# Two heads' scores and transposes, issued turn by turn on the two row halves of TensorE

## The chip, the core and the metric

The kernel runs on one core of one Trainium2 chip, as one program. The metric is the device time of an execution in microseconds; the median of three executions of the kernel before is 3099.32 us. Five engines work side by side, each through its own queue in order: TensorE (PE, with its weight loads as PEld), VectorE (DVE), ScalarE (ACT), GpSimd (POOL) and SyncE (SP), which here issues nearly all DMAs.

## What is computed

Two layers of a decoder trunk on 1024 tokens of width 1024, in float32. Layer 0 has a gated linear recurrence (Hawk) as its mixer, layer 1 RWKV-7 time mixing; each is followed by a SwiGLU block and a gated per-layer embedding. The change lies in the RWKV-7 recurrence, 16 heads of 64 channels:

```python
def step(S, inp):
    r_t, w_t, k_t, v_t, a_t, b_t = inp
    sa = jnp.einsum('bhvk,bhk->bhv', S, a_t)
    S = S * w_t[:, :, None, :] + sa[..., None] * b_t[:, :, None, :] + v_t[..., None] * k_t[:, :, None, :]
    y = jnp.einsum('bhvk,bhk->bhv', S, r_t)
    return S, y
```

The kernel doesn't step through tokens. It cuts the sequence in chunks of 64 tokens and computes, per chunk and head, the 64x64 matrices of scores between tokens, the inverse of a triangular one of them, and with these the state's step from chunk to chunk.

## The kernel before

Tokens are worked on in two halves of 512 (`t`), features lie on the partitions. The dense products (names `pg`, `pu`, `ops`, `pps`, `lps`, `lx`, `gx`, `pq`) each add up three float32r matmuls of 128x512 per block of weights, from a high and a low part of both operands. Weights are loaded by SyncE into `raw`, ScalarE casts the high part `whl` (L238) and GpSimd subtracts for the low one (L239).

The recurrence is woven into this dense work. A group `G` is four heads of a half, that is two pairs `jj` of heads; the two heads of a pair lie on partitions 0 to 63 (`E`) and 64 to 127 (`O`), and `HV` lists them. Four generators produce the work:

- `stage1` prepares a pair: decays, `BK` and `ZL`, then for each half of its eight chunks the scores `sc` (L115 by way of `mm`): four products of 64 rows by 128 columns per head, into one PSUM bank of 128x512. VectorE masks the bank in three steps, into AB, RB and ZL (L1057 to L1059). Then `bkt` (L1079): eight transposes per head into one bank, which ScalarE copies to `BKt` (L1083).
- `inverse` inverts the triangular matrices of a group: a long chain of small steps on VectorE (`X`, `W`), then `w`, `n`, `u`, `w`, `v`, 32 small products each, into banks of the same kind.
- `stage2` goes from chunk to chunk with `zu` and `y`, which have PSUM of their own. Its products already alternate between `E` and `O`.
- `norm2` normalizes with `bsum` and `yv`, into banks of the same kind, and stores the output `o`.

There are two such banks (`BANKS = 2`); `big` hands them out in turn. The order of TensorE's instructions in this part is fixed as the code emits them; the other engines are ordered by a scheduler with priorities (`ahead`). What the code emits is decided by a planner in the class `Kern`. It keeps a clock in ns, to which `mm` adds the length of each product. After each dense matmul `tick` looks at the four generators. Each has yielded a triple: a latency from its last step, which is multiplied by a slack of 3 (2.5 in the last part), whether it needs a bank, and a condition. A generator whose latency is over, whose bank (the next in turn) is planned free and whose condition holds is stepped, and no other follows for 1200 ns of that clock. `evac` plans a bank free after the time given with `big`, again times the slack. These plans set the order alone; on the chip, semaphores hold an instruction until its bank is really empty.

When the generators have ended, the memory pool of the scan is closed, and pools `ep` and `pe` with weight buffers and PSUM take its place (`K.until(lambda: not K.streams)`, `c.close()`, `extra(ctx)` in `tile_trunk`).

Of the kernel before, what the change touches and what calls it, by code (L numbers as in the profile page):

```python
# [27 lines left out]
BANKS = 2  # L28
# [25 lines left out]
class Part:  # L54
    def __init__(self, gen):
        self.gen, self.need = gen, (0.0, False, None)


class Kern:
# [61 lines left out]
    def ready(self, st):  # L121
        lat, bank, cond = st.need
        return (cond is None or cond()) and max(lat, self.bank_free[self.bank_n % BANKS] if bank else 0.0)
# [809 lines left out]
    def scan(self):  # L933
# [41 lines left out]
        def evac():  # L975

            i, t = held.pop(0)
            self.bank_free[i] = self.clock + t * self.slack
# [11 lines left out]
        def stage1():  # L990
# [15 lines left out]
            for P, (t, g, jj) in enumerate(order):  # L1006
# [23 lines left out]
                for c4 in range(0, NC, 4):  # L1030
# [18 lines left out]
                    yield 1500, True, None  # L1049
                    for hh, me, ot in HV:  # L1050
                        ps = big("sc", 1700).rearrange("p (c s) -> p c s", c=4)
                        for c in range(4):
                            self.mm(ps[:, c, :], BK[me, c4 + c, :, :].rearrange("p i s -> p (i s)"), zl[me, hh, c, :])
                        evac()
                        m3 = mask.unsqueeze(1).to_broadcast([128, 4, 128])
                        with self.ahead(AHEAD_S1):
                            nc.vector.tensor_mul(AB[me, cs, :], ps[me, :, 0:64], m3[me, :, 0:64])  # L1057
                            nc.vector.tensor_mul(rb[me], ps[me, :, 64:128], m3[me, :, 64:128])
                            nc.vector.tensor_mul(zl[ot, hh], ps[ot], m3[ot])  # L1059
                        if hh == 0:  # L1060
                            yield 0, True, None
                yield 0, True, (lambda: (G == 0 or inv[G - 1] >= 1) and (old < 0 or s2[old] == NC))
# [13 lines left out]
                for hh, me, ot in HV:  # L1076
                    ps = c3(big("bkt", 800))
                    for c in range(NC):
                        nc.tensor.transpose(ps[:, c, :], BK[me, c, :, :].rearrange("p i s -> p (i s)"), ident[me])  # L1079
                    self.clock += NC * 54  # L1080
                    evac()
                    with self.ahead(AHEAD_S1):
                        nc.scalar.copy(BKt[:, :, hh, :], ps)  # L1083
                    if hh == 0:
                        yield 0, True, None
# [366 lines left out]
```

## Time and profile before

| | |
|---|---|
| median of three runs | 3099.32 us (3097.59 to 3109.37) |
| the profiled execution: time, span | 3106.82 us, 3105.0 us |
| its mean granted TensorE clock | 0.979 of 2.4 GHz |
| TensorE busy | 2958.3 us, 95% of the span |
| VectorE, ScalarE, GpSimd busy | 1677.9, 1438.3, 1282.7 us |
| stretch of the woven recurrence | about 1130 to 2480 us |

A busy share is the part of the span in which an engine had an instruction running. TensorE's matmuls are pipelined, so their records overlap; a group's cost is read from the start of what stands before it to the start of what comes behind it. A float32 product leaves two records, a transpose or a float32r product one. In a list of waits, each row says who sat idle, until what ended, for how long in total, how often, and the longest time.

### The profile page before, as it was taken

The page shows a single profiled execution, that of the slowest core. Times are in us where ns is not written, and L with a number is a line of the kernel's source. Part 1 is how long each engine was busy: PE and PEld are TensorE (multiplying, and loading weights), DVE is VectorE, ACT ScalarE, POOL GpSimd, SP SyncE. Part 2 cuts the span into 40 slices and gives each one's busy share as a digit, 9 for nine tenths or more (in the row PEclk, how much of TensorE's full clock was granted, in tenths as well). Part 3 has the DMA queues.
Part 4 walks back from the last instruction along what each step waited for, and adds up shares of the span by engine and source line. Part 5 has one row for each costly group of instructions (what it writes and reads, how often), then busy time and mean ns, then how long its engine had stood idle before and what let it go on. Part 6 is the DMA issues. An engine that isn't in the chain of part 4 may idle for free. (4 is left out here: it accounts for less than half of the span.)

```text
span 3105.0 us, 45886 instructions
## 1 busy us (share of the span) xinstructions
PE 2958.3 (95%) x16904; PEld 2292.7 (74%) x16904; DVE 1677.9 (54%) x2950; ACT 1438.3 (46%) x2565; POOL 1282.7 (41%) x1080
## 2 busy tenths in 40 slices
PE   5999999999999999999998999999999999999998
PEld 3777778888776777777776667776767777888886
DVE  8756771111563266576678565777866456222145
ACT  5564752222555443444465774454344445322244
POOL 5111134444445444343434344434333355544445
PEclk9999999999998999999999999999999999999999
DMA  3211123333335464333323366423323252333323
GB/s 126 60 36 53 50 79 105 94 94 95 98 126 179 158 190 128 89 111 98 114 91 98 119 204 198 125 85 111 100 88 100 70 185 91 103 95 95 95 81 109
DMA packets 223968, 336.04 MB, mean 108 GB/s; under 512 B 56960, under 2 KB 75136, under 8 KB 223744
## 3 DMA queue, kind: packets, MB, share of 16 engines
q1 hardware_dynamic: 223456, 332.75, 34.9%
q8 instruction: 133, 2.18, 0.3%
q14 instruction: 91, 0.75, 0.1%
q10 hardware_dynamic: 288, 0.37, 0.0%
HBM read 278.24 MB, written 54.79 MB: 107 GB/s over the span
## 5 line engine op out<-in xcount | busy, mean ns | idle before, releaser
L239 POOL TENSOR_TENSOR whl<-raw,whl 128x512 fp32r<-128x512 f32 (+2 forms) x818 | 1061.8, 1303 | 1410.4 <-ACT whl L238 1319.8
L238 ACT CAST whl<-raw 128x512 fp32r<-128x512 f32 (+2 forms) x818 | 482.2, 593 | 851.5 <-PE ops L115 226.2
L115 PE MATMUL ops<-hid,whl 128*128 128x512 f32 x2112 | 523.8, 401 | 13.8 <-DVE hid L290 6.4
L115 PE MATMUL pg<-xn,whl 128*128 128x512 f32 (+1 forms) x2184 | 522.9, 392 | 4.4 <-ACT whl L238 1.9
L115 PEld LDWEIGHTS pg<-xn,whl 128*128 128x128 f32 x2184 | 405.2, 188 | 98.9 <-issue 4.3
L115 PEld LDWEIGHTS ops<-hid,whl 128*128 128x128 f32 x2112 | 392.6, 189 | 113.8 <-DVE hid L290 12.5
L115 PE MATMUL pu<-xn,whl 128*128 128x512 f32 x1584 | 385.9, 396 | 3.1 <-ACT xn L289 1.4
L115 PEld LDWEIGHTS pu<-xn,whl 128*128 128x128 f32 x1584 | 296.0, 189 | 72.0 <-DVE xn L290 2.1
L115 PE MATMUL pps<-mix,whl 128*128 128x512 f32 x1152 | 301.3, 412 | 11.9 <-ACT mix L289 5.1
L390 DVE TENSOR_TENSOR h<-h,ops 128x512 f32<-128x512 f32 x256 | 173.9, 685 | 210.6 <-PE ops L115 208.7
L555 DVE TENSOR_TENSOR sg<-sg,pu 128x512 f32<-128x512 f32 x88 | 60.4, 686 | 396.0 <-PE pu L115 395.4
L115 PEld LDWEIGHTS pps<-mix,whl 128*128 128x128 f32 x1152 | 217.7, 193 | 75.1 <-issue 7.7
L115 PE MATMUL pg<-raw,whl 128*128 128x512 f32 x720 | 198.0, 415 | 0.0
L115 PEld LDWEIGHTS pg<-raw,whl 128*128 128x128 f32 x720 | 134.4, 193 | 34.4 <-issue 3.8
L241 POOL TENSOR_SCALAR whl<-raw 128x512 fp32r<-128x512 f32 (+2 forms) x84 | 58.7, 704 | 217.6 <-PE rps L115 69.7
L115 PE MATMUL pu<-raw,whl 128*128 128x512 f32 x528 | 141.4, 406 | 0.0
L115 PE MATMUL rps<-xn,whl 128*128 128x512 f32 x480 | 123.4, 405 | 16.3 <-ACT xn L289 10.5
L115 PEld LDWEIGHTS rps<-xn,whl 128*128 128x128 f32 x480 | 91.9, 193 | 42.8 <-issue 12.0
L115 PE MATMUL gps<-xn,whl 128*128 128x512 f32 x480 | 117.9, 400 | 0.0
L115 PE MATMUL ops<-m,whl 128*128 128x512 f32 x480 | 114.4, 396 | 0.8 <-ACT m L289 0.8
L115 PEld LDWEIGHTS pu<-raw,whl 128*128 128x128 f32 x528 | 96.1, 188 | 23.8 <-issue 2.6
L115 PEld LDWEIGHTS gps<-xn,whl 128*128 128x128 f32 x480 | 92.3, 192 | 21.4 <-issue 0.5
(277 smaller groups left out, 4027.2 us busy)
## 6 DMA issues: line engine op xcount, KB each, us to landing
raw<-in_ffn_in SPq DMA_DIRECT2D x352, 256.0 KB, 2.6
raw<-in_ffn_out SPq DMA_DIRECT2D x152, 256.0 KB, 2.6
raw<-in_rkv SPq DMA_DIRECT2D x96, 256.0 KB, 3.0
raw<-in_ple_gate SPq DMA_DIRECT2D x64, 256.0 KB, 2.6
raw<-in_w_in SPq DMA_DIRECT2D x48, 256.0 KB, 2.8
h<-h SPq DMA_DIRECT2D x32, 256.0 KB, 3.5
raw<-in_ffn_out SPq DMA_DIRECT2D x48, 128.0 KB, 2.1
raw<-in_w_o SPq DMA_DIRECT2D x24, 256.0 KB, 2.7
```

The source lines that it names most:

```text
L115: self.nc.tensor.matmul(out, lhsT=lhsT, rhs=rhs, start=start, stop=stop)
L238: nc.scalar.copy(hl[:rows, 0, :w], raw[:rows, :w])
L239: nc.gpsimd.tensor_sub(hl[:rows, 1, :w], raw[:rows, :w], hl[:rows, 0, :w].bitcast(F32))
L241: nc.gpsimd.tensor_scalar(hl[:rows, 0, :w], raw[:rows, :w], 1.0, 0.0, ALU.mult, ALU.add)
L390: nc.vector.tensor_add(hs, hs, ps)
L555: nc.vector.tensor_mul(sg, sg, pu)
```

## The change

`need` and `ready` learn a number of banks in place of yes or no: with 2, the next two banks in turn must both be planned free. In `stage1` both heads' banks of scores are taken at once, and the four chunks are issued turn by turn for `E` and `O`; for each second one the planner's clock is set back by 200 ns. All six VectorE steps follow. The banks are planned as busy for 1000 and 2000 ns (1700 each before). The two heads' transposes alternate in the same way, banks at 500 and 900 ns (800 each before), and their planned length is `NC * 60` for both heads, where each had `NC * 54`. Two yields between the heads are gone.

```diff
-        self.gen, self.need = gen, (0.0, False, None)
+        self.gen, self.need = gen, (0.0, 0, None)
...
-        return (cond is None or cond()) and max(lat, self.bank_free[self.bank_n % BANKS] if bank else 0.0)
+        return (cond is None or cond()) and max([lat] + [self.bank_free[(self.bank_n + i) % BANKS] for i in range(int(bank))])
...
-                    yield 1500, True, None
-                    for hh, me, ot in HV:
-                        ps = big("sc", 1700).rearrange("p (c s) -> p c s", c=4)
-                        for c in range(4):
-                            self.mm(ps[:, c, :], BK[me, c4 + c, :, :].rearrange("p i s -> p (i s)"), zl[me, hh, c, :])
-                        evac()
-                        m3 = mask.unsqueeze(1).to_broadcast([128, 4, 128])
-                        with self.ahead(AHEAD_S1):
+                    yield 1500, 2, None
+
+                    pss = [big("sc", e).rearrange("p (c s) -> p c s", c=4) for e in (1000, 2000)]
+                    for c in range(4):
+                        for hh, me, ot in HV:
+                            self.mm(pss[hh][:, c, :], BK[me, c4 + c, :, :].rearrange("p i s -> p (i s)"), zl[me, hh, c, :])
+                            if hh:
+                                self.clock -= 200
+                    evac()
+                    evac()
+                    m3 = mask.unsqueeze(1).to_broadcast([128, 4, 128])
+                    with self.ahead(AHEAD_S1):
+                        for hh, me, ot in HV:
+                            ps = pss[hh]
                             nc.vector.tensor_mul(AB[me, cs, :], ps[me, :, 0:64], m3[me, :, 0:64])
                             nc.vector.tensor_mul(rb[me], ps[me, :, 64:128], m3[me, :, 64:128])
                             nc.vector.tensor_mul(zl[ot, hh], ps[ot], m3[ot])
-                        if hh == 0:
-                            yield 0, True, None
-                yield 0, True, (lambda: (G == 0 or inv[G - 1] >= 1) and (old < 0 or s2[old] == NC))
+                yield 0, 2, (lambda: (G == 0 or inv[G - 1] >= 1) and (old < 0 or s2[old] == NC))
...
-                for hh, me, ot in HV:
-                    ps = c3(big("bkt", 800))
-                    for c in range(NC):
-                        nc.tensor.transpose(ps[:, c, :], BK[me, c, :, :].rearrange("p i s -> p (i s)"), ident[me])
-                    self.clock += NC * 54
-                    evac()
-                    with self.ahead(AHEAD_S1):
-                        nc.scalar.copy(BKt[:, :, hh, :], ps)
-                    if hh == 0:
-                        yield 0, True, None
+                pss = [c3(big("bkt", e)) for e in (500, 900)]
+                for c in range(NC):
+                    for hh, me, ot in HV:
+                        nc.tensor.transpose(pss[hh][:, c, :], BK[me, c, :, :].rearrange("p i s -> p (i s)"), ident[me])
+                self.clock += NC * 60
+                evac()
+                evac()
+                with self.ahead(AHEAD_S1):
+                    for hh in range(2):
+                        nc.scalar.copy(BKt[:, :, hh, :], pss[hh])
```

In the built programs the order on TensorE moves at every group. Three places follow; `xN` counts equal instructions in a row. The first is TensorE's at the first pair of heads, among the products `pps` of the value projection, as a difference (- before, + changed).

```order
-L115 MATMUL sc<-ZL,BK 128x128 x4
-L115 MATMUL pps<-mix,whl 128x512 x6
-L115 MATMUL sc<-ZL,BK 128x128 x4
-L115 MATMUL pps<-mix,whl 128x512 x3
+L115 MATMUL sc<-ZL,BK 128x128 x8
+L115 MATMUL pps<-mix,whl 128x512 x9
 L115 MATMUL vtr<-cst,o 128x128 x4
```

The two heads' groups of four, six dense products apart, have become one group of eight. In the changed order, with the tiles' numbers, the eight begin like this: the two banks alternate.

```order
L115 MATMUL pps_8572<-mix_8256,whl_8569 128x512 x3
L115 MATMUL sc_8588<-ZL_8541,BK_8427 128x128
L115 MATMUL sc_8589<-ZL_8541,BK_8427 128x128
L115 MATMUL sc_8588<-ZL_8541,BK_8427 128x128
L115 MATMUL sc_8589<-ZL_8541,BK_8427 128x128
```

The second place is TensorE's at the first `bsum` of the program, which uses one of the two banks behind scores. Before:

```order
L115 MATMUL sc<-ZL,BK 128x128 x4
L115 MATMUL pu<-xn,whl 128x512 x14
L1079 MATMUL bkt<-cst,BK 128x64 x8
L115 MATMUL pu<-xn,whl 128x512 x3
L115 MATMUL ops<-hid,whl 128x512 x9
L1079 MATMUL bkt<-cst,BK 128x64 x8
L115 MATMUL bsum<-b,cst 128x512
```

Changed:

```order
L115 MATMUL sc<-ZL,BK 128x128 x8
L115 MATMUL pu<-xn,whl 128x512 x16
L115 MATMUL bsum<-b,cst 128x512
L115 MATMUL pu<-xn,whl 128x512 x5
L115 MATMUL ops<-hid,whl 128x512 x8
L1083 MATMUL bkt<-cst,BK 128x64 x16
```

`bsum` has moved ahead of the transposes and is now the next user of a bank behind the scores, 16 dense products later. The third place is TensorE's at the end of the scan, the last `bsum` and `yv`. Before:

```order
L115 MATMUL bsum<-b,cst 128x512
L115 MATMUL pu<-raw,whl 128x512 x11
L115 MATMUL ops<-hid,whl 128x512 x11
L115 MATMUL yv<-v,cst 128x512
L115 MATMUL ops<-hid,whl 128x512 x85
L115 MATMUL pg<-raw,whl 128x512 x24
```

Changed:

```order
L115 MATMUL bsum<-b,cst 128x512
L115 MATMUL ops<-hid,whl 128x512 x22
L115 MATMUL yv<-v,cst 128x512
L115 MATMUL ops<-hid,whl 128x512 x19
L115 MATMUL pu<-raw,whl 128x512 x24
L115 MATMUL pg<-raw,whl 128x512 x48
```

The last `yv` has moved behind by 66 dense products of the same 96, so 19 of them stand behind it; and of the two products that follow, `pu` now goes ahead of `pg`.

## Rows read from the trace of the kernel before

**Rows 1.** Busy time by engine in the recurrence's stretch; columns as headed.

```profile
core 0: us, PE busy (x) PEld busy (x) DVE busy (x) ACT busy (x) POOL busy (x), PEclk, DMA share, GB/s
...
1130.00:2480.00 1350.00, 1285.39 (x9848) 965.64 (x9847) 891.28 (x1883) 653.31 (x1330) 541.23 (x432) 0.98 0.38 115
```

**Rows 2.** Waits of TensorE there: total us, times, longest us.

```profile
PE bsum L115 <- issue: 8.9, 2, 6.2
...
PE bkt L1079 <- DVE ZL L1059: 2.3, 1, 2.3
```

**Rows 3.** Groups by line there: xcount | busy us, mean ns | idle before.

```profile
L115 PE MATMUL sc<-ZL,BK 64*128 64x128 f32 x512 | 77.3, 293 | 0.5 <-DVE b L1251 0.5
...
L1059 DVE TENSOR_TENSOR ZL<-sc,cst 64x512 f32<-64x512 f32 x64 | 44.1, 688 | 0.8
...
L115 PE MATMUL zu<-z,V 64*64 64x64 f32 x512 | 28.9, 232 | 4.7 <-DVE z L1199 4.7
...
L1057 DVE TENSOR_TENSOR AB<-sc,cst 64x256 f32<-64x256 f32 x64 | 26.9, 420 | 57.5 <-PE sc L115 56.8
...
L1079 PE MATMUL bkt<-cst,BK 64*128 64x64 f32 x256 | 22.6, 228 | 2.4 <-DVE ZL L1059 2.3
...
L1083 ACT COPY BKt<-bkt 128x512 f32<-128x512 f32 x32 | 18.5, 585 | 24.3 <-PE bkt L1079 24.1
```

**Rows 4.** Timeline of TensorE: start us, first start to last end us, instruction.

```profile
1206.19 3.02 PE L115 MATMUL pg<-xn,whl 128*128 128x512 f32 x12
1209.14 0.71 PE L1079 MATMUL bkt<-cst,BK 64*128 64x64 f32 x8
1209.78 0.50 PE L115 MATMUL pg<-xn,whl 128*128 128x512 f32 x1
...
1215.57 5.60 PE L115 MATMUL pg<-xn,whl 128*128 128x512 f32 x24
1221.01 5.60 PE L115 MATMUL pu<-xn,whl 128*128 128x512 f32 x24
...
1239.13 1.66 PE L115 MATMUL pu<-xn,whl 128*128 128x512 f32 x6
1240.72 1.16 PE L115 MATMUL sc<-ZL,BK 64*128 64x128 f32 x8
1241.80 2.35 PE L115 MATMUL pu<-xn,whl 128*128 128x512 f32 x9
```

**Rows 5.** The same, at a product with the inverse.

```profile
1278.61 1.88 PE L115 MATMUL ops<-hid,whl 128*128 128x512 f32 x7
1280.42 0.45 PE L115 MATMUL zu<-z,V 64*64 64x64 f32 x8
1280.80 2.34 PE L115 MATMUL ops<-hid,whl 128*128 128x512 f32 x9
```

**Rows 6.** Timeline of TensorE and VectorE, at the longest wait for a bank.

```profile
2249.34 1.16 PE L115 MATMUL sc<-ZL,BK 64*128 64x128 f32 x8
...
2261.09 0.69 DVE L1059 TENSOR_TENSOR ZL<-sc,cst 64x512 f32<-64x512 f32 x1
...
2261.89 2.05 PE L115 MATMUL bsum<-b,cst 128*128 128x512 f32 x2 [6.24 <-issue]
```

**Rows 7.** The stretch of that wait, columns as in rows 1.

```profile
2258.00:2273.00 15.00, 11.12 (x53) 7.72 (x53) 11.27 (x22) 5.36 (x10) 6.79 (x5) 0.66 0.24 80
```

**Rows 8.** Timeline of all engines behind the last `yv` of the scan.

```profile
2503.51 1.02 PE L115 MATMUL yv<-v,cst 128*128 128x512 f32 x2
...
2511.24 0.33 SPq L1265 DMA_DIRECT2D o<-ys  x1
...
2514.18 1.41 SPq L227 DMA_DIRECT2D raw<-in_ffn_in  x3
2514.81 1.14 ACT L289 CAST on<-on 128x512 fp32r<-128x512 f32 x2 [2.02 <-DMA o<-ys]
...
2517.82 1.15 ACT L238 CAST whl<-raw 128x512 fp32r<-128x512 f32 x2 [0.31 <-DMA raw<-in_ffn_in]
```

## The prediction

> **What bounds the kernel now.** I read the page's busy shares first, then the stretches, then the matmul engine's rows inside the stretch that the change touches. The change touches only the recurrence that is woven into dense work between about 1130 and 2480 us. TensorE is busy there for 1285.39 of 1350 us [rows 1], while VectorE, the next, has 891. Nothing but its own work and some short waits sets TensorE's pace, so an instruction's time taken off TensorE there comes off the end, unless a new wait replaces it. Idle TensorE time in the stretch is 65 us; what the planned PSUM banks cost of it is the 8.9 us before `bsum` and the 2.3 us before `bkt` [rows 2].
>
> **What a group of scores or transposes costs today.** Dense matmuls run at one pitch: 24 start at 1215.57 and the next 24 at 1221.01, 5.44 / 24 = 0.227 us each [rows 4]. Between the six `pu` that start at 1239.13 and the nine at 1241.80 lie one group of four scores (eight records, as each of these float32 products leaves two) and six dense matmuls: 2.67 - 6 x 0.227 = 1.31 us for the group [rows 4]. In the same way a group of eight transposes (eight records) costs 3.59 - 12 x 0.227 = 0.87 us [rows 4]. Each divides into the records and a fixed cost of leaving the full array for a smaller tile and coming back. From the first start to the last end a `sc` group takes 1.16 us, and one record 0.293 in the mean: seven steps are 0.87, so 0.124 each and 0.99 for eight, which leaves 0.32 fixed. For `bkt`: (0.71 - 0.228) / 7 = 0.069, 0.55 for eight, 0.32 fixed [rows 3, 4].
>
> **What two tiles side by side cost today.** The product with the inverse, `zu<-z,V`, already goes turn by turn to the two heads. Its eight records, nearly as long as those of `bkt` (0.232 us), take 0.45 us from first start to last end where `bkt` takes 0.71, so 0.22 against 0.48 for the seven steps: less than half. The whole group costs 2.19 - 7 x 0.227 = 0.60 us between dense matmuls, 0.27 less than `bkt` with as many records [rows 3 to 5]. So two heads do run at once there. But those two tiles differ in rows and in columns (64x64); the new pairs differ in rows alone and write the same 128 output partitions, in two banks. No row of the trace shows that form.
>
> **The change, term by term.** (1) Scores: 64 groups of four become 32 of eight, which alternate between the halves. If the halves overlap as `zu<-z,V` does, eight products take the record time of four: 32 x 0.99 = 31.7 us saved. From below: nothing saved. I take the full overlap, since the one row on alternating tiles shows it nearly exact. (2) Transposes: 32 groups become 16, 16 x 0.55 = 8.8 us saved, on the same condition. (3) Fixed costs: in the order of the whole program, stretches of scan work between dense matmuls fall from 334 to 306 (other small helpers are counted alike in both). The fall is less than the 48 groups that vanish, because some groups stood next to other scan work before. 28 x 0.32 = 9.0 us saved, whether the halves overlap or not. Together 49.5 us, say 50.
>
> TensorEngine's promise of overlap has a figure in the Trainium skill that speaks for less (TensorE: Matmul & The Clock Gate, section on packing small matmuls): four row tiles reach 3.07 times, not 4. If two reached the same 77%, an estimate from that page, terms 1 and 2 would give about 28 us in place of 40.5, and the sum would shrink by 12. The `zu<-z,V` rows show no such loss for two tiles, and no row shows it for row tiles.
>
> (4) **Banks.** Both heads' banks are now taken together and both must be free (`yield 1500, 2`). VectorE empties them: AB, RB and ZL, 0.42 + 0.42 + 0.69 = 1.53 us a head, 3.06 a pair [rows 3]; the RB row is like that of AB. Planned as busy are 3 x 1000 and 3 x 2000 ns where each had 3 x 1700, so the first bank's next user comes earlier. In the new order 16 of the 32 pairs are followed by a `bsum`, `yv` or `w` after 12 to 18 dense matmuls, 2.7 to 4.1 us; it needs the first bank, 1.5 us if VectorE starts at once. It often did not: the group of 2249.34 ended at 2250.50 and its ZL only at 2261.78, because VectorE had other work queued ahead, and `bsum` lost 6.24 us [rows 6]. Against that, the new VectorE order has, ahead of most pairs, only short work that was released several us before, and not the long chain of `W` and `X` steps of the inverse that stands ahead of several groups now. So the present 11.2 us may vanish, or half of the 16 places may wait 4 us more each (+32, net +21). I take no net change, and -11 to +21 for the range. The copies of `BKt` (0.585 us each on ScalarE [rows 3], the banks planned for 3 x 500 and 3 x 900 ns) have the smaller risk: the next `n` or `yv` comes six dense matmuls (1.4 us) later or more.
>
> (5) **The end of the scan.** The whole scan now finishes closer to the end of its dense cover: 19 `ops` matmuls stand behind the last `yv`, where there were 85. Then the scan's SBUF pool closes and its memory becomes weight buffers. In the trace the chain behind the last `yv`, which ends at 2504.53, is ScalarE, VectorE, GpSimd and two loads or stores: `o` is issued at 2511.24, and its reader on ScalarE is released at 2514.81, 10.3 us after the `yv` [rows 8]. Weights issued at 2514.18, three loads in a row, are cast from 2517.82, 3.6 us later [rows 8]. TensorE had 85 dense matmuls, 19 us, for that. Now 19 `ops` and 24 `pu` (43 x 0.227 = 9.8 us) lie in front of the `pg` that uses the freed memory, which cannot start before 10.3 + 3.6 + 0.6 for its cast = 14.5, or somewhat earlier if a load alone lands sooner. That is 3 to 5 us of new idle time, and some microseconds at the lower clock behind it; after the 6.24 us wait above, the granted clock was 0.66 over 15 us [rows 7], parts of it at 1.2 GHz. I take +6, from +2 to +9.
>
> Nothing is added or taken away on the other engines: the same evacuations, loads and stores, in another order. Sum: -50 + 0 + 6 = -44 us. Against the profiled execution's own 3106.8 us that is 3063. The runs' median, 3099.3, lies 7.5 below that execution, and a gain in this stretch is the same for both: 3055.
>
> **Rivals.**
> A. *The row halves don't overlap*, since they share the array's columns and the output partitions. Speaks for it: no row shows that form, only tiles that differ in columns too. Against: the halves take separate rows of the array, separate weights and separate banks, and `zu<-z,V` overlaps in weights and products alike. It leaves terms 3 and 5: -9 + 6, about 3096. An overlap in part lies between that and the forecast.
>
> B. *The banks become the bound, and the kernel slower.* The mechanism: VectorE empties the pair in series, with whatever stands ahead of it, while the plan lets the next user of the first bank come 2.7 us later; the user then holds up TensorE and all dense matmuls behind it. Speaks for it: the 6.24 us of [rows 6], and the clock behind it. If all 16 places lost that, 100 us, the time would be 3155. It decides against the change from 60 / 16 = 3.7 us a place (50% of it already makes it even), beyond what VectorE needed at many groups: it sat idle before AB for 56.8 us in all until the scores came [rows 3], so at those it started at once.
> The Trainium skill warns of this (TensorEngine Tiling (Array Packing), section on performance considerations): tiling speeds up TensorE but not the emptying of PSUM, which may become the bottleneck, and both ScalarE and VectorE should do it. Here VectorE alone empties the scores. By that rule the time would be B's; the trace so far bears it out at two places of 64, with 8.9 us.
>
> C. *The planner's shifted order brings waits elsewhere*, say at the start of the dense stage behind the first part, or between the products of the recurrence, whose spacing stays as it was. As the stretch's other idle time is some 50 us in many short pieces, a change by half of it is the most I would give: 3055 +- 25. It widens the range and is part of the forecast's case.
>
> **How the numbers follow.** Forecast 0.76, around 3055, its own range 3036 (bank waits vanish, the end costs 2) to 3085 (bank waits +21, the end +9, or a part of the overlap missing). A 0.09. B 0.15, of which 0.07 past the point of slower and the rest about even. Of the forecast's share I leave a few hundredths below 3036. The range 3036 to 3090 holds about 0.78. Half a percent, 15.5 us, is about what a measurement of this kernel can tell from no change: below 3083.8 faster, above 3114.8 slower. Faster 0.77; same 0.16 (A, and the weaker part of B); slower 0.07.
>
> **What would show it.** Right: `sc` groups of 16 records that last about 1.2 us from first start to last end, `bkt` groups of 16 with 0.7; TensorE's busy time some 45 us less in a stretch shorter by as much; a wait of `pg` of 4 us or so behind the last `yv`. Rival A: the groups last about 2.1 and 1.2 us. Rival B: waits of `bsum`, `yv` and `w` on ZL with tens of microseconds in the sum, and a lower clock behind them. The prediction is wrong if the groups shrink as said and the span doesn't: then the waits of TensorE name the place.

## The result, and the profile after

The changed kernel takes 3119.56 us (median of four runs, 3118.62 to 3121.24) where the kernel before takes 3100.57 in the same series: a ratio of 1.0057, 95% interval 1.0036 to 1.0078. It is slower by half a percent, 19 us; forecast were 3055 us, with 3090 as the upper end of the range. The profiled execution of the changed kernel has a span of 3119.3 us (before 3105.0).

The groups shrank as foreseen. Timeline of TensorE in the changed kernel, columns as in [rows 4]:

```profile
1137.15 3.89 PE L115 MATMUL pps<-mix,whl 128*128 128x512 f32 x16
1140.97 1.16 PE L115 MATMUL sc<-ZL,BK 64*128 64x128 f32 x16
1142.06 2.11 PE L115 MATMUL pps<-mix,whl 128*128 128x512 f32 x8
...
1203.82 1.29 PE L115 MATMUL pg<-xn,whl 128*128 128x512 f32 x5
1205.05 0.71 PE L1083 MATMUL bkt<-cst,BK 64*128 64x64 f32 x16
1205.69 4.60 PE L115 MATMUL pg<-xn,whl 128*128 128x512 f32 x19
```

Sixteen records of scores now last 1.16 us, sixteen transposes 0.71, to the hundredth what eight lasted before [rows 4]. Between dense matmuls the pair costs 1142.06 - 1137.15 - 16 x 0.227 = 1.28 us, where one head alone cost 1.31.

The stretch between 1130 and 2480 us, columns as in [rows 1]:

```profile
1130.00:2480.00 1350.00, 1246.60 (x9780) 932.88 (x9779) 894.34 (x1859) 652.66 (x1323) 533.04 (x429) 0.96 0.38 116
```

TensorE is busy for 1246.60 us there instead of 1285.39 [rows 1], yet it is no further in the program; the granted clock fell from 0.98 to 0.96. The waits of TensorE name what came in (total us, times, longest, whole execution), beside [rows 2]:

```profile
PE nps L115 <- DVE acc L301: 27.2, 8, 12.3
PE sc L115 <- DVE b L1255: 11.6, 4, 7.4
PE bsum L115 <- DMA b<-b: 11.0, 1, 11.0
...
PE yv L115 <- ACT v L1256: 8.4, 3, 6.5
...
PE w L115 <- DVE ZL L1065: 4.7, 3, 2.9
PE pg L115 <- ACT xn L289: 4.4, 2, 4.0
```

Two thirds of the first row are old. The kernel before, whole execution:

```profile
PE nps L115 <- DVE acc L301: 18.5, 7, 12.3
```

Two new kinds stand out; the kernel before has 0.5 us of the one and nothing of the other. The first is `sc` waiting for `b`: a pair of scores needs both banks, so also the one that `bsum` of the norm has filled and VectorE must empty. Timeline of TensorE and VectorE in the changed kernel at the longest of them (in brackets: idle time, releaser):

```profile
2270.34 1.02 PE L115 MATMUL bsum<-b,cst 128*128 128x512 f32 x2
...
2274.90 1.30 DVE L1132 TENSOR_TENSOR X<-X,W 128x28 f32<-128x28 f32 x1
...
2280.98 0.68 DVE L1255 SCALAR_TENSOR_TENSOR b<-bsum,v 128x512 f32<-128x512 f32 x1
...
2281.71 2.07 PE L115 MATMUL sc<-ZL,BK 64*128 64x128 f32 x14 [7.40 <-DVE b L1255]
```

`bsum` was done at 2271.4; VectorE worked, with one pause of 0.25 us, on the inverse's chain, dense steps and the next head's preparation and emptied the bank only at 2281.7. The clock over this place, columns as in [rows 1]:

```profile
2276.00:2287.00 11.00, 5.29 (x23) 4.41 (x24) 8.87 (x19) 6.79 (x13) 5.13 (x6) 0.53 0.31 89
```

The second is not a bank at all. Timeline of the changed kernel at the 11.0 us:

```profile
1721.97 1.20 POOL L1266 TENSOR_SCALAR ys<-ys,vec 128x512 f32<-128x512 f32 x1
...
1723.21 0.69 DVE L1267 TENSOR_TENSOR ys<-ys,b 128x512 f32<-128x512 f32 x1 [0.68 <-POOL ys L1266]
...
1723.93 0.33 SPq L964 DMA_DIRECT2D b<-b  x1
...
1726.69 2.08 PE L115 MATMUL bsum<-b,cst 128*128 128x512 f32 x2 [11.02 <-DMA b<-b]
```

The bonus `b` of the next head is loaded into one of two tiles, and the older one is in use until `ys` of the head ahead has had it added. The load is issued right behind that step and lands under 3 us later; `bsum` had stood in TensorE's queue for 11 us by then, with all dense work behind it.

**One account for all runs.** To compare kernels I split each profiled span in three. Idle is the span less TensorE's busy time (part 1 of the page). Half clock is half of the time at 1.2 GHz in which TensorE was busy, summed over the trace's stretches at that level: an estimate of what the lower level cost while there was work. Work is the rest. Idle holds some 7.3 us behind TensorE's last instruction, which the expectations below leave out (139 for the kernel before).

| kernel | median us | ratio to before, 95% | span | idle | half clock | work |
|---|---|---|---|---|---|---|
| before | 3100.6 to 3104.8 by series | 1 | 3105.0 | 146.8 | 55.5 | 2902.8 |
| after | 3119.6 | 1.0036 to 1.0078 | 3119.3 | 189.2 | 72.9 | 2857.3 |
| e1 serial | 3125.3 | 1.0051 to 1.0096 | 3120.7 | 178.2 | 62.6 | 2879.9 |
| e2 long | 3098.9 | 0.9980 to 1.0004 | 3096.8 | 171.8 | 70.6 | 2854.4 |
| e3 clock | 3107.6 | 1.0005 to 1.0028 | 3106.9 | 184.1 | 66.4 | 2856.3 |
| e4 tight | 3124.5 | 1.0046 to 1.0099 | 3119.9 | 158.9 | 55.7 | 2905.4 |
| e5 prio | 3110.4 | 1.0010 to 1.0031 | 3110.9 | 184.2 | 67.0 | 2859.7 |
| e6 long, prio | 3118.5 | 1.0032 to 1.0062 | 3116.6 | 188.3 | 73.0 | 2855.4 |
| e7 scores only | 3116.5 | 1.0031 to 1.0061 | 3115.4 | 177.7 | 67.5 | 2870.2 |
| e8 transposes only | 3134.5 | 1.0088 to 1.0118 | 3131.2 | 179.4 | 57.5 | 2894.3 |
| e9 before, gap 1000 | 3121.8 | 1.0035 to 1.0068 | 3107.6 | 152.7 | 49.5 | 2905.5 |
| e10 before, gap 1400 | 3128.1 | 1.0063 to 1.0093 | 3128.1 | 168.3 | 58.3 | 2901.5 |
| e11 after, gap 1000 | 3110.9 | 1.0012 to 1.0031 | 3110.7 | 180.6 | 73.2 | 2856.9 |
| e12 after, gap 1400 | 3103.0 | 0.9990 to 1.0010 | 3099.4 | 188.3 | 53.9 | 2857.2 |
| e13 after, ScalarE helps | 3119.7 | 1.0033 to 1.0067 | 3123.3 | 193.8 | 71.3 | 2858.2 |
| e14 before, ScalarE helps | 3112.6 | 1.0021 to 1.0043 | 3110.3 | 154.0 | 52.7 | 2903.6 |
| e15 after, gap 1400, long | 3121.2 | 1.0036 to 1.0067 | 3120.6 | 194.3 | 68.8 | 2857.5 |
| e16 before, less dense | 3085.5 | 0.9931 to 0.9964 | 3083.5 | 167.3 | 61.5 | 2854.7 |
| e17 before, scores twice | 3164.4 | 1.0182 to 1.0218 | 3171.2 | 136.2 | 75.2 | 2959.8 |
| e18 after, less dense | 3087.2 | 0.9928 to 0.9961 | 3084.9 | 202.3 | 75.1 | 2807.5 |

For the change it reads: work -45.5, idle +42.4, half clock +17.4, together +14.3. The work went away; more than it came back as waiting. The account is of one execution each, and a kernel's own runs lie 3 to 20 us apart (that of e9 is the fastest of its six, 12 us under their median, that of e17 the slowest of four, 9 us above); what is said of faster and slower goes by the medians and ratios.

### The profile page after: what moved, and what is told of

Read it like the earlier page. It is cut to its first block, busy times and chain, and to the rows that moved or that the text cites. A ratio compares the mean times of both kernels' runs of the same rounds, so it can differ in the third digit from the quotient of the medians.

```text
span 3119.3 us, 45834 instructions
## 1 busy us (share of the span) xinstructions
PE 2930.1 (94%) x16904; PEld 2264.7 (73%) x16904; DVE 1689.8 (54%) x2950; ACT 1440.0 (46%) x2565; POOL 1277.1 (41%) x1080
## 5 line engine op out<-in xcount | busy, mean ns | idle before, releaser
L115 PEld LDWEIGHTS ops<-hid,whl 128*128 128x128 f32 x2112 | 390.8, 189 | 117.5 <-DVE hid L290 14.5
L115 PE MATMUL rps<-xn,whl 128*128 128x512 f32 x480 | 123.3, 405 | 16.0 <-ACT xn L289 10.2
L115 PEld LDWEIGHTS rps<-xn,whl 128*128 128x128 f32 x480 | 91.9, 193 | 42.2 <-issue 11.7
L1207 ACT ACTIVATE ss<-SV,PC 64x64 f32<-64x64 f32 x240 | 82.9, 345 | 76.5 <-DVE SV L1224 60.2
```

The costliest lines, as they stand in the source:

```text
L115: self.nc.tensor.matmul(out, lhsT=lhsT, rhs=rhs, start=start, stop=stop)
L1207: nc.scalar.activation(ss[me], SV[me, c, hh, :], AF.Copy, scale=PC[me, c : c + 1])
```

## The experiments

One thing holds for all runs below: what the planner fixes is the order on TensorE alone. The scheduler orders the other engines anew for every kernel, also where TensorE's order stays. By the traces, at least 236 of VectorE's 2950 instructions and 78 of SyncE's 1382 loads and stores stand elsewhere in e16 than in the kernel before, 170 and 43 in e17; against the changed kernel it is 172 and 18 in e1, 162 and 25 in e5, 220 and 77 in e18. (The count is the fewest that have to be moved to turn one order into the other.) So no run changes TensorE's work and nothing else.

**First series: is the overlap real, and are the banks' times the cause?** e1 keeps the plan of the changed kernel and its order of groups on TensorE, and issues the heads of a pair one after the other.

```diff
-                    for c in range(4):
-                        for hh, me, ot in HV:
+                    for hh, me, ot in HV:
+                        for c in range(4):
...
-                for c in range(NC):
-                    for hh, me, ot in HV:
+                for hh, me, ot in HV:
+                    for c in range(NC):
```

> The changed kernel with the same plan and the same order of groups on TensorE, but inside a group the four (or eight) products of one head go first and then those of the other, so the two row halves can't run at once. This undoes the overlap alone. If the overlap is real (theory and rival agree on that): a scores group of 16 records costs about 2.2 us between dense matmuls instead of 1.29, a transposes group 1.4 instead of 0.83, some 32 x 0.95 + 16 x 0.55 = 39 us more TensorE work, and 3140 to 3165 us, since part of the added time falls into waits that are there anyway. If the change's slowness came from the overlap itself not helping: the time stays at 3120.

Measured: 3125.3 us. The work rose by 2879.9 - 2857.3 = 22.6 us, not 39, and the time by some 5 to 6. Both parts teach something. Timeline of e1 on TensorE, at the place shown above:

```profile
1136.56 3.90 PE L115 MATMUL pps<-mix,whl 128*128 128x512 f32 x16
1140.38 1.71 PE L115 MATMUL sc<-ZL,BK 64*128 64x128 f32 x16
1142.02 2.11 PE L115 MATMUL pps<-mix,whl 128*128 128x512 f32 x8
```

Sixteen records one head after the other take 1.71 us, and between dense matmuls 1142.02 - 1136.56 - 3.63 = 1.83; two separate groups cost 2 x 1.31 = 2.62 before. So joining the groups saves 0.79 us a pair, the turn-by-turn order another 0.55. And where 22 us of work come back with TensorE's order unchanged, only a quarter of it shows in the time: idle fell by 11 us and the half clock by 10. That is a first sign that TensorE's work alone does not set the end here, and no more than a sign: VectorE's order moved too, and the intervals of the two kernels overlap.

e2 lengthens the planned bank times of the changed kernel:

```diff
-                    pss = [big("sc", e).rearrange("p (c s) -> p c s", c=4) for e in (1000, 2000)]
+                    pss = [big("sc", e).rearrange("p (c s) -> p c s", c=4) for e in (1700, 3000)]
...
-                pss = [c3(big("bkt", e)) for e in (500, 900)]
+                pss = [c3(big("bkt", e)) for e in (800, 1400)]
```

e3 takes back only the planner's shorter clock in the changed kernel:

```diff
-                            if hh:
-                                self.clock -= 200
...
-                self.clock += NC * 60
+                self.clock += NC * 108
```

e4 shortens the bank times in the kernel before, without pairs:

```diff
-                        ps = big("sc", 1700).rearrange("p (c s) -> p c s", c=4)
+                        ps = big("sc", 1000).rearrange("p (c s) -> p c s", c=4)
...
-                    ps = c3(big("bkt", 800))
+                    ps = c3(big("bkt", 500))
```

> The changed kernel with the banks of a pair planned as busy for longer: scores 3 x 1700 and 3 x 3000 ns instead of 3 x 1000 and 3 x 2000, transposes 3 x 800 and 3 x 1400 instead of 3 x 500 and 3 x 900. Theory (the gain is lost to users of the two banks that stand in TensorE's queue before VectorE and ScalarE have emptied them): the waits of sc, w, yv, bkt on these banks fall from about 28 us to 10 or less, the time at 1.2 GHz falls with them, and the time is 3080 to 3100 us. Rival (any shift of the planner's order brings new waits of other kinds, for loads, for the dense products' inputs, and the bank waits are only one kind among them): the bank waits fall, others come, 3105 to 3135.

> The changed kernel with the overlap, but the planner's own clock counts both halves' products in full (no set-back of 200 ns a product, 108 ns for each pair of transposes instead of 60), as it did before. The bank times are those of the change, and both banks are still taken at once. Theory (short bank times and both banks at once): bank waits stay at 20 us or more, 3105 to 3125 us. Rival (the planner's shifted clock is what hurt): waits fall back to those of the kernel before, and with 50 us less work the time is 3060 to 3085.

> The kernel before, heads one by one and no overlap, with shorter bank times alone: scores 3 x 1000 instead of 3 x 1700 ns, transposes 3 x 500 instead of 3 x 800. Theory: short bank times by themselves bring 10 to 25 us more waits of bank users and half-clock time: 3110 to 3130 us. Rival: the order is shaken without a direction, 3090 to 3110, and the bank waits stay near the 12 us of the kernel before.

Measured: 3098.9, 3107.6 and 3124.5. e3 came out in the range of its theory, far from the 3060 to 3085 of the rival, though 12 us below the changed kernel. Alone, e2 and e4 would make a neat story: longer times win 21 us, shorter ones cost 23. But e2 only comes level with the kernel before, at 48 us less work, and its list of waits shows why the story is too neat:

```profile
PE sc L115 <- DVE b L1255: 12.1, 3, 7.3
PE bsum L115 <- DMA b<-b: 11.3, 3, 6.3
```

The two new kinds of wait are as long as in the changed kernel; what fell is spread over many others. In e4 the waits of `bsum` are those of before (8.7 us; [rows 2] has 8.9), and what rose is of other kinds:

```profile
PE bsum L115 <- issue: 8.7, 2, 5.1
...
PE gx L115 <- DVE whl L823: 8.5, 2, 5.9
PE lps L115 <- ACT whl L238: 7.3, 2, 5.1
```

These are dense products that wait for their weights. The tight times moved the order, and the loss came elsewhere than at the banks.

**Second series: does the remedy add up, and which half of the change is it?** e5 leaves TensorE's order as it is in the changed kernel and puts the steps that empty the banks ahead of others in their engines' queues; e6 adds the longer times of e2:

```diff
-AHEAD_DENSE, AHEAD_S1, AHEAD_INV, AHEAD_S2 = 600, 300, 600, 1200
+AHEAD_DENSE, AHEAD_S1, AHEAD_INV, AHEAD_S2 = 600, 1000, 600, 1200
```

e7 is the diff of the change with only its hunks on the scores (the transposes and the yield ahead of them as before), e8 the diff with only its hunks on the transposes.

> The changed kernel with TensorE's order untouched; alone the steps that empty the two banks (the masks of the scores, BKt, and those of norm2) are put ahead of the inverse's and the dense steps in the other engines' queues (an urgency of 1000 instead of 300, where the inverse and the dense steps have 600). Theory, sharpened by the runs so far (TensorE waits since a releaser of a bank stands behind other work in VectorE's queue, as the b of 2280.98 us behind ten microseconds of inverse and dense steps): the waits of sc, yv, w, bkt on these banks fall from about 34 us to under 12, the half-clock time with them, and the time falls to 3085 to 3105. Rival (the plan's order as such, with loads and dense inputs late): these waits fall, but others take their place, 3110 to 3130.

> Both remedies at once: the longer planned bank times (3 x 1700 and 3 x 3000, 3 x 800 and 3 x 1400) and the higher urgency of the steps that empty the banks. Theory: together they leave only waits that the kernel before had too, and the 50 us of saved TensorE work show: 3060 to 3085 us. Rival: no better than the longer times alone, 3090 to 3110, with waits on loads and on the dense products' inputs instead.

> The change to the scores alone; the transposes are issued head by head with the bank times of before. Theory: nearly all of the loss sits with the scores, since their banks are emptied by VectorE over 3 us a pair: 3105 to 3125 us. Rival (order): anything from 3080 to 3130, with waits of kinds other than the banks'.

> The change to the transposes alone; the scores are issued head by head with the bank times of before. Sixteen groups of 0.83 us vanish, 13 us of TensorE work. Theory: their banks are emptied by ScalarE in 1.2 us a pair, little is given back: 3085 to 3097 us. Rival (order): 3085 to 3120.

Measured: 3110.4, 3118.5, 3116.5, 3134.5. e5 won 9 us, but `sc` still waited 13.3 us for `b`:

```profile
PE sc L115 <- DVE b L1255: 13.3, 4, 7.4
...
PE bsum L115 <- DMA b<-b: 9.1, 1, 9.1
```

The higher urgency did not bring `b` forward enough. e6, with both remedies, is 20 us slower than e2 alone (17 by the ratios of their series). And e8, with the smaller half of the change, 8.4 us less work and scores as before, is the slowest of all but e17: 33 us more idle time than before, of which one wait of 11.7 us for the same load of `b`. e7 lies in the ranges of theory and rival alike, e6 and e8 above both. The theory of the bank times falls with these; the rival, that any new order costs, gained, though it had the cost too low twice.

**Third series: is the plan of before a favourable one?** One number of the planner, the least time between two steps of a stream, is moved in both kernels alike, to 1000 in e9 (before) and e11 (after), to 1400 in e10 (before) and e12 (after):

```diff
-PACE = ((3, 1200), (2.5, 200))
+PACE = ((3, 1000), (2.5, 200))
```

> The kernel before with one number of its plan moved and no other change: at least 1000 ns instead of 1200 between two steps of a stream. It has the TensorE work of before (2906 us of its span is neither idle nor lost to the half clock; idle is 139). Two readings are open after the first eight runs, in which every new plan had 150 to 181 us of idle time. P: the plan of before is a lucky or tuned one, and any shift of it costs 15 to 40 us of waits, with or without pairs: this run gives 3115 to 3140. T: the waits come from the pairs, since TensorE is now faster than the engines that feed it: this run gives 3090 to 3108, with idle time of 130 to 145.

> The kernel before with 1400 ns instead of 1200 between two steps of a stream, the other direction. P: 3115 to 3140, idle time 150 to 175. T: 3090 to 3108, idle time 130 to 145.

> The changed kernel with 1000 ns instead of 1200 between two steps of a stream, beside the same shift of the kernel before. P: it has 45 us less TensorE work and waits like those of the shifted kernel before, so 3070 to 3100, some 40 below it. T: 3110 to 3130, idle time 170 to 185 again, above the shifted kernel before.

> The changed kernel with 1400 ns instead of 1200 between two steps of a stream. P: some 40 us below the kernel before with 1400, 3070 to 3105. T: 3110 to 3130, idle time 170 to 185.

Measured: before 3121.8 and 3128.1, after 3110.9 and 3103.0. With either number the kernel with pairs is the faster one, by 11 and by 25 us, and with 1200 the slower one by 19. The kernel before loses 19 and 25 us from a step in either direction: its own plan sits in a hollow. Still P, as expected there, is only half right, since the paired kernels are not 45 us below their partners: they have 28 and 20 us more idle time each, and the 3110.9 of e11 lies in the range of T (which had it above its partner, not below).

**Fourth series: is it VectorE's load?** The RB third of the scores' banks is emptied by ScalarE and masked by GpSimd, with TensorE's order untouched, in e13 for the changed kernel and in e14 for the kernel before. e15 joins the two plan figures that had helped the changed kernel, 1400 in PACE and the bank times of e2.

```diff
-                            nc.vector.tensor_mul(rb[me], ps[me, :, 64:128], m3[me, :, 64:128])
+                            nc.scalar.copy(rb[me], ps[me, :, 64:128])
+                            nc.gpsimd.tensor_mul(rb[me], rb[me], m3[me, :, 64:128])
```

> The changed kernel with TensorE's order untouched; a third of the emptying of the scores' banks leaves VectorE: ScalarE copies the RB part out of PSUM and GpSimd masks it in SBUF, 64 steps of 0.42 us (27 us) less on VectorE, a bank's emptying on VectorE 1.1 us instead of 1.53. T (TensorE now runs ahead of VectorE's queue): idle time falls from 181 us to 150 to 165 and the time to 3085 to 3105. Against T (the waits are the plan's, of no engine in particular): 3112 to 3130, or slower since ScalarE and GpSimd get longer queues.

> The control: the same move of RB from VectorE to ScalarE and GpSimd in the kernel before, with its order on TensorE untouched. T: VectorE is less often late there, so the gain is smaller than with pairs: 3090 to 3103. Against T: it moves by as much as the changed kernel does, either way.

> The changed kernel with both plan figures that helped it one at a time: 1400 ns between steps of a stream and the longer planned bank times (3 x 1700 and 3 x 3000, 3 x 800 and 3 x 1400). If plan figures add up: 3080 to 3095, which would beat both kernels. If each plan is a draw of its own, as the longer times with the higher urgency suggested (3118 where each alone gave less): 3100 to 3120.

Measured: 3119.7, 3112.6, 3121.2. VectorE's busy time in the stretch fell from 894 to 873 us in e13, and the waits on it didn't:

```profile
PE sc L115 <- DVE b L1256: 17.1, 4, 9.2
PE yv L115 <- ACT v L1257: 13.3, 3, 12.0
```

That `b` stands behind other work in VectorE's queue, as in the timeline of 2280.98 us, and that a shorter queue in the mean does not move it forward, would fit this; it was not tested by itself. The Trainium skill (TensorEngine Tiling (Array Packing), section on performance considerations) advises to use both ScalarE and VectorE for the copy out of PSUM, as it may become the bottleneck. Here the changed kernel gained nothing from it (3119.7 against 3119.6 us), and the kernel before took 9 us longer, each with a new order on VectorE. e15 took back what each of its two figures had won.

**Fifth series: what is TensorE's work worth here?** This is the first step of the prediction, tested with TensorE's order held. e16 and e18 leave out every sixth of the third dense products while the scan runs, while the plan counts them; e17 issues each product of the scores twice and counts it once. TensorE's order, the banks and the planned times stay those of the kernel that they start from; the orders of the other engines do not, as said above. e16 (220 matmuls fewer) and e18 (224):

```diff
-                    self.mm(ps, wl, xh, False, i == len(pairs) - 1)
+                    if skip:
+                        self.clock += 512 / 2.4
+                    else:
+                        self.mm(ps, wl, xh, False, i == len(pairs) - 1)
```

e17:

```diff
-                        for c in range(4):
+                        for c in (0, 1, 2, 3) * 2:
                             self.mm(ps[:, c, :], BK[me, c4 + c, :, :].rearrange("p i s -> p (i s)"), zl[me, hh, c, :])
+                        self.clock -= 4 * 128 * 4 / 2.4
```

> The kernel before with 220 dense matmuls left out, every sixth of the third products (weight remainder times input) while the scan runs, so its output is a little less exact; the plan counts them as if they were there, so the order of all else, the banks and their planned times stay. That takes 220 x 0.227 = 50 us of work off TensorE, as much as the change does, but spread evenly and without a word on banks. If the stretch were bound by TensorE's work, as the prediction said: 3050 to 3060 us. If the work saved turns into waits whoever saves it, since TensorE's queue is held by other engines often enough: 3080 to 3100, with idle time up from 139 to 165 to 185. If only savings in the scores and transposes are lost: 3050 to 3065.

> The other direction: the kernel before with every product of the scores issued twice into the same place, the plan counting them once, so order and planned times stay. That is 64 groups of eight more records, 64 x 0.11 x 8 = 56 us or somewhat more of TensorE work. Bound by TensorE's work: 3155 to 3170. If waits take part of it up: 3115 to 3140, with idle time under 139.

> The changed kernel with the same every sixth third product left out while the scan runs (224 matmuls, 51 us; the output a little less exact), order and plan as they are. Bound by TensorE's work: 3065 to 3075. If the work saved turns into waits: 3095 to 3115, idle time 195 or more.

Measured: 3085.5, 3164.4, 3087.2. In e16, 48.1 us of work went and the time fell by 18 us (11 to 21 by the interval): idle rose by 20.5 us (to 160 as the expectation counts it, which had 165 to 185), the half clock by 6.0. So about two fifths of the work taken away shows. From the changed kernel the same cut took 32 us off, two thirds of 49.8. In e17, 57.0 us of work came in and the time rose by 61, but not by the work one for one: in its trace idle fell by 10.6 us and the half clock rose by 19.7, and in e1 only a quarter of the added work showed. Work and time are not one for one here in either direction. Whether a cut turns into waits since TensorE then comes early, or since the other engines' new order brings their work late, these runs do not separate.

Where e16 lost it, by its waits:

```profile
PE nps L115 <- DVE acc L306: 21.8, 8, 12.3
...
PE bsum L115 <- issue: 9.6, 2, 7.8
PE pg L115 <- ACT xn L294: 8.2, 1, 8.2
```

The wait of `pg` for `xn` is the start of a dense stage, whose input is loaded in parts by SyncE and cast on ScalarE. The changed kernel has 4.0 us of it, the kernel before 0.8 (behind the step on VectorE that follows the cast). Timeline of the kernel before:

```profile
1156.32 0.90 SPq L714 DMA_DIRECT2D xn<-xn  x2
...
1157.46 4.58 PE L115 MATMUL pg<-xn,whl 128*128 128x512 f32 x19
...
1160.12 0.62 ACT L289 CAST xn<-xn 128x512 fp32r<-128x512 f32 x1 [3.62 <-DMA xn<-xn]
```

And of e16:

```profile
1154.46 4.13 PE L115 MATMUL pg<-xn,whl 128*128 128x512 f32 x17
...
1161.49 0.91 SPq L719 DMA_DIRECT2D xn<-xn  x2
...
1166.17 0.62 ACT L294 CAST xn<-xn 128x512 fp32r<-128x512 f32 x1 [8.28 <-DMA xn<-xn]
```

TensorE came 3.0 us earlier, but the last two loads were issued 5.2 us later and the cast began 6.1 us later. Most of this wait is not TensorE's earliness: the loads stand elsewhere in SyncE's queue.

The waits between 1130 and 2640 us, summed by kind from the trace (bank users are `sc`, `bkt`, `bsum`, `yv` and the products of the inverse; others are mostly `lps`, `gx`, `lx` and `vtr`):

| kernel | bank users | load of `b` | `pg`, `pu`, `ops`, `pps` | `nps` | recurrence `zu` | others | sum |
|---|---|---|---|---|---|---|---|
| before | 22.9 | 0 | 24.9 | 3.4 | 7.8 | 11.7 | 70.7 |
| e16 | 28.6 | 0 | 34.3 | 6.7 | 10.0 | 10.6 | 90.3 |
| e2 | 25.1 | 11.3 | 33.7 | 11.3 | 6.1 | 9.0 | 96.4 |
| after | 38.2 | 11.0 | 34.6 | 12.1 | 8.2 | 10.9 | 115.2 |

Of the 44.5 us that the change added, these dense products and `nps` have 18.4, where e16, with TensorE's order held, added 12.7, the wait for `xn` among them. The other 26 are bank users and the load of `b`, of which e16 added 5.7. So waits of both kinds come with less work, and the larger part of those at the banks and at `b` only with TensorE's new order; how much of each is a TensorE that comes early is not shown.

## Why the prediction was wrong, point by point

**The work.** Terms 1 to 3 gave -49.5 us; measured -45.5. The sum held, its parts did not: joining the groups gave 2902.8 - 2879.9 = 22.9 us where term 3 had 9.0, and the overlap 22.6 where terms 1 and 2 had 40.5. I had split a group into records and a fixed cost of 0.32 us and took eight records of the second head, without overlap, as another full 0.99 us. But heads issued one after the other overlap in part by themselves. Timeline of e17, where all sixteen records use one row half:

```profile
1132.06 2.05 PE L115 MATMUL sc<-ZL,BK 64*128 64x128 f32 x16
```

2.05 us in one half, 1.71 in two halves one after the other (e1), 1.16 turn by turn. Rival A was thereby priced wrongly too: without overlap by turns the work still falls by 23 us, not 9. The estimate of 28 us from the Trainium skill (TensorE: Matmul & The Clock Gate, packing small matmuls) rested on a loss among tiles that two row halves don't show here: sixteen records last as long as eight.

**The first step.** "An instruction's time taken off TensorE there comes off the end, unless a new wait replaces it": this is the step that failed. I read it from the busy share, 1285 of 1350 us [rows 1]. The clause on new waits was there, but the sum asked for them at two places only, with 0 at the banks and +6 at the end of the scan, and left the others to rival C, as likely a gain as a loss. Measured are 42.4 us of new idle time and 17.4 at the half clock against the 45.5 of work saved. e16 shows the like where TensorE's order was held: of 48.1 us of work, 18 came off the end. The reading of this that I find likeliest is that a queue that is 95% busy can be so because each dependent step elsewhere is just covered by it, so that less work uncovers many at once. It is argued and not shown, since the other engines' orders moved with every cut.

**Term 4, the banks.** I took no net change and -11 to +21; the waits of bank users rose by 15.3, within that (15.2 without the rows in which `yv`, `n` and `w` wait for an input). Which ones, I had wrong: rival B had `bsum`, `yv` and `w` waiting for the scores' ZL (`yv` and `w` did, 7.3 us), but the largest kind is the scores waiting for `b` (11.6), because a pair takes both banks. My text said that both must be free and priced only the banks' next users. (The lower end of my range, 3036, does not follow from its terms, which give 3055 - 11 - 4 = 3040; nothing hangs on it.)

**Rival C, the shifted order.** It was a part of the forecast's case with at most 25 us, "half" of the stretch's other idle time. It was worth more: less the waits of bank users (15.3) and the one at the end (3.0), 24 us of new idle time are left for it, 11.0 of them the load of `b`, and the half clock comes on top. How far order and plan move the time, the series show: nine paired kernels with nearly the same work, 2854 to 2860 us, run from 3098.9 to 3121.2, 3112 in the mean; five kernels with heads one by one and the full work run from 3101 to 3128, 3118 in the mean. The mean gain of the pairs is 6 us, with 30 us more idle time and 14 more at the half clock against 47 less work; beside a scatter (standard deviation) of 8 us among the nine and 11 among the five, 6 us is too little to count as shown. The kernel before is the fastest of its five, and the change was tried at one of its own worse plans.

**Term 5, the end of the scan**, came at the low end of its range (+6, from +2 to +9): the wait was there, the lower clock behind it was not; from 2480 to 2570 us the granted clock was 1.00. Timeline of the changed kernel behind the last `yv`, beside [rows 8]:

```profile
2526.97 1.02 PE L115 MATMUL yv<-v,cst 128*128 128x512 f32 x2
...
2533.70 0.33 SPq L1269 DMA_DIRECT2D o<-ys  x1
2535.84 2.18 ACT L289 CAST on<-on 128x512 fp32r<-128x512 f32 x4 [6.45 <-DMA o<-ys]
...
2540.12 0.70 PE L115 MATMUL pg<-raw,whl 128*128 128x512 f32 x2 [2.34 <-issue]
...
2541.49 4.70 PE L115 MATMUL pg<-raw,whl 128*128 128x512 f32 x19 [0.67 <-POOL whl L239]
```

`pg` starts 12.1 us behind the end of `yv` and waited 3.0 us in all, where I had 14.5 and 3 to 5.

**The clock.** It had no term of its own but a few microseconds at the end. It cost 17.4 us more than before, beside the waits that it stood behind.

**What stays open.** The cause of the new waits: how many come from less work on TensorE and how many from new orders on it and on the other engines; a cut with every queue's order held was not run. Why the plan of before lies some 10 to 25 us below its neighbours, and whether a plan for pairs exists that keeps the two fifths that e16 kept: none of the nine was faster than the kernel before beyond its interval. How much of the bank users' waits belongs to taking both banks at once could not be separated, since a pair issued by turns writes both; a third bank was not tried.

## What to carry to other kernels

A high busy share does not say that removed work will show. Before pricing a cut, look at how much later each releaser could have come, or cut a like amount of work elsewhere with the order held fixed: e16 is nearly that test, and its 18 us of 48 would have warned of the gain, though not foretold a loss of 19. Then compare the order of every queue, and not of the changed one alone: here the scheduler moved the others. Where an order is planned by a table of figures, compare two versions over several plans of each; one plan against one plan here gave the opposite sign of two others.

## What was not expected of the hardware

Two row halves given eight products each, one half after the other, took 1.71 us where the same half with sixteen took 2.05, so the second half began before the first was through its queue. And the lower clock lasted very differently around waits of like length. At the wait of `bsum` that the kernel before has too [rows 6, 7], with 8.2 us of idle time in place of 6.2, e17 had this over 25 us (columns as in [rows 1]):

```profile
2312.00:2337.00 25.00, 18.63 (x85) 14.16 (x87) 13.09 (x22) 4.70 (x8) 5.98 (x5) 0.52 0.19 53
```

A granted clock of 0.52, nearly all of it at 1.2 GHz, against 0.66 over 15 us before; TensorE had work for 18.6 of the 25 us. The stretch at 1.2 GHz lasted 23.9 us there, 17.1 in e16 at the same place (a wait of 7.8 us), 10.2 in the kernel before (6.2) and 10.2 in the changed kernel at its wait for `b` (7.4). Why is open; more work is not the reason, as e16 has less than the kernel before.
